# A hybrid retention and attention block on one core: made products dealt over heads and pairs, output weights loaded ahead

## The chip, the core and the metric

One core of a Trainium2 chip runs the whole kernel. The metric is the device time of one execution in microseconds (us), the median over runs.

## What is computed

One layer of an encoder block on 1024 positions and 16 meta tokens put before them (T = 1040), width 1024, all in float32. Cut to what matters:

```python
u = rms_norm(h, pre_w)
rq, rk, rv, rg, aq, ak, av, ag, gr, ga = split(u @ w_in)         # 1024 -> 7680
# branch A: retention, 4 heads, key size 128, value size 256, chunks of 128
o_r = retention_forward(rq, rk, rv) + retention_backward(rq, rk, rv)   # two scans over chunks
y_r = (group_norm(o_r) * ret_nw * silu(rg)) @ w_rb
# branch B: attention in a window of +-128, 8 heads in 2 groups, meta keys always seen, a sink logit
y_a = (softmax_attention(rotary(aq), rotary(ak), av, sink) * silu(ag)) @ w_ab
out = (sigmoid(gr) * y_r + sigmoid(ga) * y_a) @ w_o
return h + rms_norm(out, post_w)                                  # meta tokens dropped
```

## The kernel before

Every float32 product is three TensorE matmuls (`mm3`, lines 69 to 73): each operand is split into a high part (a rounded copy, by ACT or POOL) and a low part (the rest, by VectorE, `dve_lo`), and high x high, low x high and high x low add up in one PSUM bank. So each new operand costs a copy and a VectorE subtraction before TensorE can use it.

The program runs through these stages:

1. The keys and queries of head 0 (`qk0_mm`), while the input loads.
2. Retention, heads 0 to 3 (`retention`). For each chunk `stage1` projects the values (`pv`), transposes keys (`tr`), and `stage2` makes the inner product (`pa`), the chunk's state (`pkv`) and the forward scan (`Sf`). Then a loop runs back over the chunks: the backward state `Sb` is split by POOL and VectorE, one product `pb` uses it, VectorE adds it to the output and takes the statistics of the group norm, and `finish` turns the normed chunk (`to`). While this runs, `fill` gives out pieces of other work, one call of 8 pieces in each backward chunk. A piece is one step of a projection's sum, mostly three matmuls. For heads 0 to 2 these are the next head's key and query projections (`gen_qk`, 48 pieces); for head 3 the first attention keys, products, and attention queries.
3. Attention in four pairs of heads (`attention(hp, fill)`, `hp` 0 to 3), eight blocks of 128 queries each. For a block, `stage1` makes two scores (`ps`; the last matmul of each goes into the list `scored`), softmax runs over VectorE, ACT and POOL, `stage2` turns the probabilities (`pt`), `stage3` multiplies by the values (`po`). After `stage2(n)`, `fill(FILL[hp][n])` gives out pieces: query projections of this pair and the next (`gen_aq`), keys of the second group (`gen_ak`), and products.
4. Four large products by a scheme with 7 instead of 8 half-size products per pair of output blocks: z (gates, 16 units `u`), r and a (the two branches), o (output). `run` walks through all their products in one list of jobs; `prepare` splits the operands six jobs (`LEAD`) ahead; `combine` copies or adds results out of their banks (`copy` on ACT, `plus` on VectorE); `hooks` are functions called after a certain job: `refill` loads and splits the right-hand operand of the next phase, and `pre_split(k)` forms four differences of blocks of the output weights, splits them and stores them for phase o.

**Made products.** `PRE` says which products of the z phase are made early, as filling: product 2, and for some units 3. `gen_pre(u)` loads the weights into `wr` tiles, forms the difference for product 3 with three VectorE operations (`we`, lines 709 to 711), splits (`weh`, `wel`), and then gives 4 pieces of three 128x512 matmuls for each product (`pe`), copies it out and stores it in `e_d`. The z phase loads it back and adds it, and skips the job. Before, there are 22 such products. `all_pre` is one generator, `pre`, for all; `pieces(pre, n)` gives out the next n pieces. In the kernel before, heads 1 to 3 take them by `between`, called in `stage2` behind the forward product of chunks 0 to 3; head 3 takes 16 more by `fill`; pair 3 takes the rest.

**What sets the order.** Instructions are put in order for each engine by a scheduler that works on the traced program with its own estimate of times; each engine then runs its list in that order. `tc.issue_after(ins)` puts the instructions of its block that run on `ins`'s engine behind `ins`. Tiles are rings: a tag with `bufs=n` has n buffers, and a new tile waits until the readers of the one n before it are done. PSUM has 8 banks: 3 for projections and products (`pj`), 2 `p1` (transposes), 2 `p2` (scores, `pkv`), 1 `p3` (`pa`, `pb`, `po`). SP issues nearly all DMAs, in order.

Of the kernel before, what the change touches and what calls it, by code (L numbers as in the profile page):

```python
# [8 lines left out]
R = mybir.dt.float32r  # L9
AF = mybir.ActivationFunctionType  # L10
ALU = mybir.AluOpType
# [11 lines left out]
PIECES = [(0, 272), (272, 528), (528, 784), (784, 1040)]  # L23
HALVES = [(16, 528), (528, 1040)]
MW = 416
FILL = {**{h: (8, 8, 0, 8, 8, 8, 8, 0) for h in range(3)}, 3: (16, 16, 0, 14, 10, 8, 8, 0)}
PRE = {u: (2, 3) if u > 7 else (2,) for u in range(2, 16)}

U_QK, U_V, U_G = 0, 4, 8
U_AK, U_AV, U_AQ, U_AG = 12, 13, 14, 18  # L30
# [8 lines left out]
def block_kernel(ctx: ExitStack, tc: tile.TileContext, xT, x, w_in, w_rb, w_ab, w_out, vecs, dec, sink,  # L39
                 post_w, rope, tab, out):  # L40
    nc = tc.nc
# [198 lines left out]
    with tc.tile_pool(name="setup", bufs=1, reuse_waits="tile") as st:  # L240
# [61 lines left out]
        for k in range(KT):  # L302
            t = xr[k]
# [127 lines left out]

    pend = []

    def retention(h, fill, between):
        q, kt = qk[h]
        qh, ql = [], []
        for i in range(2):
# [62 lines left out]
        def stage2(c):  # L500
            n, vh, vl, kd, s = st1.pop(c)
            if c > 0:
                fh, fl = state["fs"]
                pa = p3(f"pa{h}_{c}")
                mm3(pa[:, 0:256], s[0], s[1], vh, vl, True, True)
                mm3(pa[:, 256:512], qs(qh, c), qs(ql, c), fh, fl, True, True)
                o = op[c - 1]
                nc.scalar.activation(o, pa[:, 0:256], AF.Copy, scale=rcol[:, c:c + 1])
                nc.vector.scalar_tensor_tensor(o, pa[:, 256:512], qdf(h, c), o, op0=ALU.mult, op1=ALU.add)
            if kd:  # L510
                pk = p2(f"pkv{h}_{c}")
            if "f" in kd:
                a, b = kd["f"]
                forward = mm3(pk[:, 0:256], a[0:n], b[0:n], vh[0:n], vl[0:n], True, True)
                if h and c < 4:

                    with tc.issue_after(forward):
                        between(h // 3 + 1)
                new = rp.tile([P, 256], F32, tag="S", bufs=2, name=f"Sf{h}_{c}")
                if c == 0:  # L520
                    nc.vector.tensor_copy(new, pk[:, 0:256])
                else:
                    nc.vector.scalar_tensor_tensor(new, state["f"], cdf(h), pk[:, 0:256], op0=ALU.mult, op1=ALU.add)
                state["f"] = new
                state["fs"] = split_state(new, f"f{h}_{c}")
            if "b" in kd:
                a, b = kd["b"]
                mm3(pk[:, 256:512], a, b, vh, vl, True, True)
                nc.scalar.copy(kvb[c - 1], pk[:, 256:512])
# [150 lines left out]
            nc.vector.tensor_tensor(x[o], x[a], x[b], ALU.subtract)  # L680
            nc.sync.dma_start(xs_d[n][k], x[o])

    def pre_split(k, tile_, src):

        x = {}
        for i, j in ((0, 0), (0, 1), (1, 1), (1, 0)):
            x[i, j] = t = gtile(f"w{i}{j}{k}")
            src(t, 4 * i + k, j)
        for n, o, a, b in SUMS:
            nc.vector.tensor_tensor(x[o], x[a], x[b], ALU.subtract)  # L690
            h, l = (tile_(f"w{n}{k}{e_}", s, R) for s, e_ in enumerate("hl"))
            nc.scalar.copy(h, x[o])
            nc.sync.dma_start(pre_d[n][0][:, k], h.bitcast(F32))
            dve_lo(l, x[o], h)
            nc.sync.dma_start(pre_d[n][1][:, k], l.bitcast(F32))

    gates = [U_G + u for u in range(4)] + [U_AG + u for u in range(4)] + [U_GR + u for u in range(8)]

    def gen_pre(u):
# [29 lines left out]
    def pieces(gen, n):  # L729

        for _ in range(n):
            yield next(gen)
# [9 lines left out]
        decay_table((0,))  # L742
        evac_qk0(3, 5)
    for h in range(NH):
        fill, drain = filler([*([gen_qk(h + 1)] if h < 3 else [gen_ak(0), pieces(pre, 16), gen_aq(0, 0)])])
        if h == 0:
            with tc.issue_after(normed):
                nc.vector.tensor_tensor(qd, rcol[:, 1:9].unsqueeze(1).to_broadcast([P, 2 * NH, NB]),
                                        dtab[:, 8:16].unsqueeze(2).to_broadcast([P, 2 * NH, NB]), ALU.mult)
        with tc.issue_after(rotated):  # L750
            retention(h, fill, filler([pieces(pre, (0, 4, 4, 8)[h])])[0])
            drain()
    while pend:
        pend.pop(0)()
# [19 lines left out]
    def gtile(name):  # L774
        return gp.tile([P, 512], F32, tag="g", bufs=6, name=name)
# [6 lines left out]
    class Phase:  # L782
# [96 lines left out]
        def combine(self, u, p, st):  # L879
            def new(tag):  # L880
                return (lp if tag == "c1" else yp).tile([P, 512], F32, tag=tag, bufs=2, name=f"{tag}{self.nm}{u}")

            def copy(tag):
                st[tag] = new(tag)
                nc.scalar.copy(st[tag], st["X"][0])  # L885

            def plus(o, i, at):
                nc.vector.tensor_tensor(o, i, st[at][0], add)
                return o

            def done(at):
                free.append(st[at][1])

            apart, early = u in self.apart, u in self.early
            if p == 1:
                copy("c1")
                e = self.e.pop((u, 2), None)
                if e is not None:
                    nc.vector.tensor_tensor(st["c1"], st["c1"], e, add)
                    self.post(u, 0, 0, st["c1"])  # L900
            elif p == 6 and (u, 3) in self.e:
                st["u2"] = new("u2")
                plus(st["u2"], self.e.pop((u, 3)), "X")
                self.post(u, 0, 1, plus(st["u2"], st["u2"], "Y"))
            elif p == 2:
                self.post(u, 0, 0, plus(st["c1"], st["c1"], "Z"))
                done("Z")
            elif p == 6:
                copy("u2")
                if (self.nm, u) == last[:2]:  # L910
                    plus(st["u2"], st["u2"], "Y")
                if apart:
                    done("X")
                    st["u3"] = plus(new("u3"), st["u2"], "W")
                if early:
                    plus(st["u2"], st["u2"], "V")
                    done("V")
                    self.post(u, 0, 1, plus(st["u2"], st["u2"], "Y"))
            elif p == 7 and not apart:
                copy("u3")  # L920
                if (self.nm, u) == last[:2]:
                    done("X")
            elif p == 3 and (self.nm, u) == last[:2]:
                self.post(u, 0, 1, plus(st["u2"], st["u2"], "V"))
                done("V")
            elif p == 3 and not early:
                self.post(u, 0, 1, plus(new("c5") if apart else st["u2"], st["u2"], "Y"))
                done("Y")
            elif p == 4 and apart:
                self.post(u, 1, 0, plus(st["u2"], st["u2"], "W"))  # L930
                done("W")
            elif p == 4:
                self.post(u, 1, 0, st["X"][0], new("c5"))
                done("X")
            if "u3" in st and "Y" in st and "c22" not in st:
                st["c22"] = plus(new("c5") if (self.nm, u) == last[:2] else st["u3"], st["u3"], "Y")
                self.post(u, 1, 1, st["c22"])
                if early or 3 in self.pre.get(u, ()) or (self.nm, u) == last[:2]:
                    done("Y")
# [20 lines left out]
    def refill(nm, src):  # L960
# [38 lines left out]
        def got(n):  # L999
            return lambda: get_pre(n)  # L1000

        if nm == "z":
            return {-16: [load(0, 0), load(0, 1)], -13: [load(1, 1)], -11: [plain("B22", 1, 1)],
                    -9: [plain("B11", 0, 0)], -7: [t1, load(1, 0)], -5: [t2, t3], -4: [b21], -3: [plain("T3", 0, 1)],
                    -1: [plain("T4", 0, 0)]}
        if nm == "a":
            return {-16: [load(0, 0)], -14: [load(1, 1)], -13: [plain("B11", 0, 0)], -11: [got("T1")],
                    -10: [load(1, 0)], -9: [got("T2")], -7: [plain("B21", 1, 0)], -5: [got("T3")],
# [5 lines left out]
    def run(phases):  # L1014

        jobs = [(ph, u, p) for ph, _ in phases for u, p in ph.seq]
        hooks, i = {}, 0
        for ph, src in phases:
            i += len(ph.seq)
            if src:  # L1020
                hooks.update({i + j: f for j, f in refill(ph.nm, src).items()})
        for k in range(4):
            hooks[10 * k + 30] = [lambda k=k: pre_split(k, stage, act_src(w_out))]
        n = 0
        for i, (ph, u, p) in enumerate(jobs):
            while n < min(i + LEAD, len(jobs)):
                q, u_, p_ = jobs[n]
                q.prepare(u_, p_)
                n += 1
            yield  # L1030
            ph.product(u, p)
            for f in hooks.get(i, ()):
                f()
# [174 lines left out]
    def attention(hp, fill):  # L1208
# [110 lines left out]
        for n in range(NB):  # L1319
# [7 lines left out]
                yield  # L1327
            stage2(n)
            if hp < 3 or n < NB - 2:
                fill(FILL[hp][n])  # L1330
            if hp in (1, 2) and n in (2, 5):
                sum_row(2 * hp - 2 + n // 3)
            if n >= NB - 2:
# [10 lines left out]
                nc.sync.dma_start(out[P * r:P * r + 2 * P], x[P * r:P * r + 2 * P])  # L1344

    def fills(hp):
        l = [gen_aq(hp, 1)]
        if hp == 2:
            l.insert(0, gen_ak(1))
        if hp < 3:  # L1350
            l.append(gen_aq(hp + 1, 0))
        else:
            l.append(pre)
        return l

    del wak[:]
# [112 lines left out]
```

## Time and profile before

| | before |
|---|---|
| median of 3 runs | 1125.66 us (1124.36 to 1126.15) |
| the profiled execution, its own time | 1122.79 us |
| its span, first to last instruction | 1120.5 us |
| mean granted TensorE clock | 0.978 |
| busy: PE / VectorE (DVE) / ACT / POOL | 1077.5 / 887.9 / 510.3 / 217.9 us |

The profile is of one execution. PE is TensorE, PEld its weight loads, DVE VectorE, SPq the queue of SyncE. Matmuls overlap their neighbours, so the sum of their durations is more than the time they take; from start to start is the better measure. The granted clock is the share of TensorE's full clock that the chip let through. Idle time of an engine is listed with what ended it.

### The profile page before, as it was taken

To read this page: it belongs to the slowest core of one execution; us is meant where nothing else is said; L and a number is where in the kernel's file an instruction comes from. 1 tells how busy PE (TensorE), PEld (TensorE's weight loads), DVE (VectorE), ACT (ScalarE), POOL (GpSimd) and SP (SyncE) were. 2 spreads that over 40 slices of the span, in tenths; PEclk is the share of its full clock that TensorE was granted. 3 is DMA by queue.
4 is the path that set the end of the run, shared out by engine and by line. 5 is a ranking of instruction groups with operands and counts; after the bars stand their busy time and mean duration, and the time that the engine had idled before them with its cause. 6 is when DMAs were issued, how large, how long until landed. Compare 5 with 4: busy or idle time off the path is not lost.

```text
span 1120.5 us, 17075 instructions
## 1 busy us (share of the span) xinstructions
PE 1077.5 (96%) x5939; PEld 924.8 (83%) x5939; DVE 887.9 (79%) x1797; ACT 510.3 (46%) x1128; POOL 217.9 (19%) x276
## 2 busy tenths in 40 slices
PE   8998998998999999999998999999999899999997
PEld 7897897997988988987886788878887688787786
DVE  7888579587788498789756798798989989876765
ACT  7141442322432455554567644445555536433442
POOL 3334224133134244432210000000000000010032
PEclk9999799898999999999999999999999999999998
DMA  7111111102124274233524757699995664789463
GB/s 281 38 67 38 39 58 57 48 20 66 49 87 131 66 251 133 73 129 119 191 104 153 242 175 264 183 357 334 327 359 166 249 207 151 234 193 337 147 113 75
DMA packets 84533, 176.73 MB, mean 158 GB/s; under 512 B 8880, under 2 KB 23728, under 8 KB 83632
## 3 DMA queue, kind: packets, MB, share of 16 engines
q1 hardware_dynamic: 80560, 169.09, 44.1%
q0 software_dynamic: 3456, 6.29, 3.7%
q8 instruction: 46, 0.75, 0.3%
q10 hardware_dynamic: 432, 0.28, 0.1%
q14 instruction: 39, 0.32, 0.1%
HBM read 120.57 MB, written 58.20 MB: 160 GB/s over the span
## 4 chain that ended last, share of the span: by engine, by line
PE 50%; DVE 13%; DMA 7%; issue 3%; ACT 3%; SPq 0%; DVEq 0%; POOL 0%; POOLq 0%; ACTq 0%
PE bz L71 4%; PE bz L72 4%; PE bz L73 4%; PE bo L72 2%; PE bo L71 2%; PE bo L73 2%; PE br L72 2%; PE br L73 2%; PE ba L72 2%; PE br L71 2%; PE ba L73 2%; PE ba L71 2%; PE paq L71 2%; PE paq L72 2%; PE paq L73 2%
## 5 line engine op out<-in xcount | busy, mean ns | idle before, releaser
L1106 POOL DMA_DIRECT2D mx_d<-c1a x4 | 3.7, 917 | 405.2 <-DVE c1a L1097 405.2
L71 PE MATMUL bz<-T,lhz 128*128 128x512 f32 x192 | 76.6, 399 | 2.8 <-ACT u3z L885 2.2
L71 PE MATMUL pv<-wh,big 128*128 128x256 f32 x256 | 75.2, 294 | 1.2 <-DVE m_qk L164 1.2
L73 PE MATMUL bz<-T,lhz 128*128 128x512 f32 x192 | 76.3, 398 | 0.0
L72 PE MATMUL bz<-T,llz 128*128 128x512 f32 x192 | 76.2, 397 | 0.0
L73 PE MATMUL pv<-wl,big 128*128 128x256 f32 x256 | 74.9, 293 | 0.0
L72 PE MATMUL pv<-wh,big 128*128 128x256 f32 x256 | 74.7, 292 | 0.0
L72 PE MATMUL bz<-big,llz 128*128 128x512 f32 x168 | 66.7, 397 | 0.0
L71 PE MATMUL bz<-big,lhz 128*128 128x512 f32 x168 | 66.4, 399 | 0.0
L73 PE MATMUL bz<-big,lhz 128*128 128x512 f32 x168 | 66.3, 396 | 0.0
L1255 DVE CUSTOM_DVE_ANT_0 raw<-ps,mask,nsink 128x400 f32<-128x400 f32 (+1 forms) x64 | 37.9, 595 | 25.3 <-ACT p L1258 24.4
L1267 POOL TENSOR_SCALAR p<-p,den 128x400 f32<-128x400 f32 (+1 forms) x60 | 39.6, 674 | 81.4 <-DVE den L1261 66.2
L71 PEld LDWEIGHTS pv<-wh,big 128*128 128x128 f32 x256 | 51.0, 199 | 2.2 <-DVE m_qk L164 1.5
L1258 ACT ACTIVATE p<-raw,nm 128x401 f32<-128x401 f32 (+1 forms) x64 | 38.8, 606 | 28.5 <-PE pt L1284 16.7
L72 PEld LDWEIGHTS pv<-wh,big 128*128 128x128 f32 x256 | 50.8, 198 | 0.8
L72 PE MATMUL paq<-big,wl 128*128 128x512 f32 x128 | 51.0, 398 | 0.0
L71 PE MATMUL paq<-big,wh 128*128 128x512 f32 x128 | 50.8, 397 | 0.0
L73 PE MATMUL paq<-big,wh 128*128 128x512 f32 x128 | 50.7, 396 | 0.0
L73 PEld LDWEIGHTS pv<-wl,big 128*128 128x128 f32 x256 | 50.6, 198 | 0.0
L566 ACT ACTIVATE ost<-to,rnw 128x128 f32<-128x128 f32 x64 | 20.0, 364 | 61.9 <-PE to L561 56.9
L71 PEld LDWEIGHTS bz<-T,lhz 128*128 128x128 f32 x192 | 36.6, 190 | 12.0 <-ACT u3z L885 2.6
L72 PEld LDWEIGHTS bz<-T,llz 128*128 128x128 f32 x192 | 36.6, 191 | 8.5
(631 smaller groups left out, 3691.0 us busy)
## 6 DMA issues: line engine op xcount, KB each, us to landing
wrz<-in_w_in_dram SPq DMA_DIRECT2D x32, 512.0 KB, 5.8
wr<-in_w_in_dram SPq DMA_DIRECT2D x29, 512.0 KB, 3.8
e<-e SPq DMA_DIRECT2D x44, 256.0 KB, 4.2
we<-in_w_in_dram SPq DMA_DIRECT2D x16, 512.0 KB, 3.6
tg<-tg_d SPq DMA_DIRECT2D x32, 256.0 KB, 4.6
T<-preT SPq DMA_DIRECT2D x6, 1024.0 KB, 7.6
oTr_d<-ost SPq DMA_DIRECT2D x16, 256.0 KB, 2.1
xs<-in_xT_dram SPq DMA_DIRECT2D x8, 512.0 KB, 3.5
```

Of the source, the lines that this page charges most:

```text
L71: nc.tensor.matmul(o, ah, bh, start=first, stop=False, **kw)
L72: nc.tensor.matmul(o, al, bh, start=False, stop=False, **kw)
L73: return nc.tensor.matmul(o, ah, bl, start=False, stop=last, **kw).ins
L566: nc.scalar.activation(ost[0][:, e_, w0:w0 + P], to[:, P * e_:P * e_ + P], AF.Copy, scale=rnw[:, 2 * h + e_:2 * h + e_ + 1])
L1106: nc.gpsimd.dma_start(d, to, accum_op=ALU.add)
L1255: nc.vector.tensor_tensor_reduce(raw[e_][:, 1:1 + wid], s[:, 0:wid], mask[:, mo:mo + wid], -SCALE, nsink[:, hd:hd + 1], ALU.add, ALU.min, ...
L1258: nc.scalar.activation(p[:, 0:1 + wid], raw[e_][:, 0:1 + wid], AF.Exp, scale=-1.0, bias=nm_[:, e_:e_ + 1], accum_out=den[:, e_:e_ + 1])
L1267: nc.gpsimd.tensor_scalar(pt[e_][:, 0:wid], pt[e_][:, 0:wid], den[:, e_:e_ + 1], 1.0, op0=ALU.mult, op1=ALU.mult)
```

## The change

- 20 made products instead of 22. `PRE` now holds product 2 of units 2 to 13 and product 3 of units 6 to 13; units 14 and 15 do all 7 products in the z phase.
- In retention `between` is gone. Products follow in the same `fill`: 4, 4 and 8 pieces behind the key and query projections of the next head for heads 0, 1 and 2; 8 for head 3, between keys and queries of attention.
- In attention each pair has its own row in `FILL`, and products in its list: 8, 16, 0 and 32 pieces, for pair 0 and 1 between this pair's queries and the next pair's. Each fill now stands in `tc.issue_after(scored[-5])`, the second score of the block before, once there are five.
- `pre_split` is cut in two. `pre_load(k)` issues the four loads of output weights six jobs before `pre_split(k)`, into the `sg1` ring of 8 buffers (`stage(..., 1)`) instead of the `g` ring of 6. The subtractions stand behind the latest `plus`, which `near` keeps. The hooks come after jobs 16, 28, 40 and 52 (loads) and 22, 34, 46 and 58 instead of 30, 40, 50 and 60.
- `refill` has no branch of its own for z any more; z takes the general one, whose steps lie over the last 16 jobs in another order.

```diff
-FILL = {**{h: (8, 8, 0, 8, 8, 8, 8, 0) for h in range(3)}, 3: (16, 16, 0, 14, 10, 8, 8, 0)}
-PRE = {u: (2, 3) if u > 7 else (2,) for u in range(2, 16)}
+FILL = (6, 5, 5, 5, 5, 5, 5, 4), (6,) * 8, (6, 5, 5, 4, 4, 4, 4, 0), (7, 7, 7, 7, 6, 6, 8)
+PRE = {u: (2, 3) if u > 5 else (2,) for u in range(2, 14)}
...
-                forward = mm3(pk[:, 0:256], a[0:n], b[0:n], vh[0:n], vl[0:n], True, True)
-                if h and c < 4:
-
-                    with tc.issue_after(forward):
-                        between(h // 3 + 1)
+                mm3(pk[:, 0:256], a[0:n], b[0:n], vh[0:n], vl[0:n], True, True)
...
-    def pre_split(k, tile_, src):
-
-        x = {}
+    def pre_load(k, src):
+
+        w[k] = {}
         for i, j in ((0, 0), (0, 1), (1, 1), (1, 0)):
-            x[i, j] = t = gtile(f"w{i}{j}{k}")
+            w[k][i, j] = t = stage(f"w{i}{j}{k}", 1)
             src(t, 4 * i + k, j)
+
+    def pre_split(k, behind):
+
+        x = w.pop(k)
         for n, o, a, b in SUMS:
-            nc.vector.tensor_tensor(x[o], x[a], x[b], ALU.subtract)
-            h, l = (tile_(f"w{n}{k}{e_}", s, R) for s, e_ in enumerate("hl"))
+            with tc.issue_after(behind):
+                nc.vector.tensor_tensor(x[o], x[a], x[b], ALU.subtract)
+            h, l = (stage(f"w{n}{k}{e_}", s, R) for s, e_ in enumerate("hl"))
...
-        fill, drain = filler([*([gen_qk(h + 1)] if h < 3 else [gen_ak(0), pieces(pre, 16), gen_aq(0, 0)])])
+        fill, drain = filler([gen_qk(h + 1), pieces(pre, (4, 4, 8)[h])] if h < 3 else [gen_ak(0), pieces(pre, 8), gen_aq(0, 0)])
...
-            retention(h, fill, filler([pieces(pre, (0, 4, 4, 8)[h])])[0])
+            retention(h, fill)
...
             def plus(o, i, at):
-                nc.vector.tensor_tensor(o, i, st[at][0], add)
+                near[:] = [nc.vector.tensor_tensor(o, i, st[at][0], add).ins]
                 return o
...
-        if nm == "z":
-            return {-16: [load(0, 0), load(0, 1)], -13: [load(1, 1)], -11: [plain("B22", 1, 1)],
-                    -9: [plain("B11", 0, 0)], -7: [t1, load(1, 0)], -5: [t2, t3], -4: [b21], -3: [plain("T3", 0, 1)],
-                    -1: [plain("T4", 0, 0)]}
...
         for k in range(4):
-            hooks[10 * k + 30] = [lambda k=k: pre_split(k, stage, act_src(w_out))]
+            hooks[12 * k + 16] = [lambda k=k: pre_load(k, act_src(w_out))]
+            hooks[12 * k + 22] = [lambda k=k: pre_split(k, near[0])]
...
             if hp < 3 or n < NB - 2:
-                fill(FILL[hp][n])
+                with tc.issue_after(scored[-5]) if len(scored) > 4 else ExitStack():
+                    fill(FILL[hp][n])
...
-        l = [gen_aq(hp, 1)]
+        l = [gen_aq(hp, 1), pieces(pre, (8, 16, 0, 32)[hp])]
         if hp == 2:
             l.insert(0, gen_ak(1))
         if hp < 3:
             l.append(gen_aq(hp + 1, 0))
-        else:
-            l.append(pre)
```

More of the change, by code (lines that the diff above doesn't have):

```diff
@@ L432, in block_kernel, with retention @@
     pend = []
-    def retention(h, fill, between):
+    def retention(h, fill):
         q, kt = qk[h]
@@ L695, in pre_split @@
             nc.sync.dma_start(pre_d[n][1][:, k], l.bitcast(F32))
+    w, near = {}, []
     gates = [U_G + u for u in range(4)] + [U_AG + u for u in range(4)] + [U_GR + u for u in range(8)]
```

## The prediction, made before the changed kernel had run

> **What bounds the kernel now.** I read the page first, for the engine that is never free and for its clock.
>
> ```profile
> span 1120.5 us, 17075 instructions
> PE 1077.5 (96%) x5939; PEld 924.8 (83%) x5939; DVE 887.9 (79%) x1797; ACT 510.3 (46%) x1128; POOL 217.9 (19%) x276
> PE   8998998998999999999998999999999899999997
> PEclk9999799898999999999999999999999999999998
> ```
>
> TensorE is the bound, and both programs hold the same matmuls, so time can only come from two places: microseconds in which PE stands idle, and microseconds in which its clock is granted by half. The PEclk slices show that the second kind sits where the first is. So I cut the span into stretches by the windows view (columns: window and length, then busy us and count of PE, PEld, DVE, ACT, POOL, then the mean granted clock, DMA share, GB/s).
>
> ```profile
> 40.00:98.00 58.00, 58.00 (x442) 55.38 (x442) 47.76 (x118) 16.26 (x48) 22.90 (x28) 1.00 0.10 33
> 98.00:118.00 20.00, 13.52 (x78) 10.42 (x77) 18.80 (x54) 5.12 (x16) 10.92 (x16) 0.74 0.24 79
> 98.00:126.00 28.00, 21.52 (x115) 17.68 (x113) 20.64 (x59) 6.11 (x19) 11.40 (x17) 0.70 0.20 66
> 186.00:206.00 20.00, 16.24 (x91) 14.13 (x90) 12.59 (x35) 5.70 (x18) 4.90 (x8) 0.74 0.15 54
> 264.00:282.00 18.00, 14.55 (x84) 12.59 (x83) 10.68 (x32) 5.13 (x17) 4.25 (x7) 0.81 0.18 58
> 282.00:316.00 34.00, 34.00 (x273) 33.26 (x272) 25.38 (x65) 15.75 (x42) 5.02 (x9) 1.00 0.20 64
> 487.00:556.00 69.00, 67.43 (x366) 56.47 (x365) 58.55 (x114) 34.74 (x90) 19.63 (x21) 1.00 0.43 142
> 582.00:613.00 31.00, 26.23 (x153) 21.85 (x153) 18.55 (x49) 22.80 (x63) 4.71 (x8) 0.94 0.33 113
> 740.00:751.00 11.00, 8.80 (x32) 6.71 (x31) 8.73 (x16) 5.18 (x10) 0.00 (x0) 0.84 1.00 345
> 856.00:890.00 34.00, 29.94 (x120) 23.28 (x119) 32.69 (x55) 19.02 (x34) 0.00 (x0) 0.95 0.68 236
> 890.00:1030.00 140.00, 140.00 (x603) 113.03 (x602) 114.06 (x186) 60.61 (x107) 8.86 (x10) 1.00 0.69 214
> ```
>
> I price a stretch at its idle time plus (1 - clock) times its length, as if PE had work through all of its half-rate time. The tails of heads 0, 1 and 2: 6.5 + 8.4 = 14.9, 3.8 + 5.2 = 9.0, 3.4 + 3.4 = 6.8; 30.7 in all. The last blocks of attention (582 to 613): 4.8 + 1.9 = 6.7. In the z phase (740 to 751): 2.2 + 1.8 = 4.0. From z to r (856 to 890): 4.1 + 1.7 = 5.8. Between these PE is busy throughout at full clock. A 128x512 matmul costs 140 / 603 = 0.232 us; the window 740:751 also gives the smallest dose of half clock, 0.16 x 11 = 1.8 us, drawn by one wait of 2.2.
>
> Now the tail of head 0 in order of time, PE alone (start, duration, instruction; in brackets the idle time before it and what ended it).
>
> ```profile
> 102.91 0.28 PE L71 MATMUL pv<-wh,big 128*128 128x256 f32 x1
> 103.03 0.28 PE L72 MATMUL pv<-wh,big 128*128 128x256 f32 x1
> ...
> 104.99 0.36 PE L71 MATMUL pb<-Shb,qh 128*128 128x256 f32 x1 [1.22 <-DVE rs L591]
> 107.10 0.35 PE L71 MATMUL pb<-Shb,qh 128*128 128x256 f32 x1 [1.29 <-DVE op L585]
> 109.49 0.55 PE L71 MATMUL pb<-Shb,qh 128*128 128x256 f32 x1 [1.80 <-DVE op L585]
> 116.24 0.66 PE L561 MATMUL to<-ident,op 128*128 128x128 f32 x2 [1.30 <-DVE op L593]
> 117.62 0.48 PE L468 MATMUL tr<-ident,kr 128*128 128x128 f32 x1 [0.50 <-ACT ost L566]
> 119.39 0.80 PE L71 MATMUL pe<-big,weh 128*128 128x512 f32 x1
> ```
>
> Value projections (`pv`) run 0.12 us apart, then stop at 103.0; each backward step waits for VectorE; and the made product of that head (`pe`) starts only at 119.39, since `between` put it behind the forward product of head 1. It takes its `pj` bank, one of three, in turn before the third `pv` tile. That is what keeps projections out of the gap.
>
> **The tails.** The change takes `between` away and lets products follow the projections in `fill`. In the order of the new program's matmuls the tail of head 0 holds, from its first `pb` to the first `tr` of head 1, 7 matmuls of a product and 152 of `pv` tiles 0 to 6, where before it held 35 of `pv`: (152 - 35) x 0.12 + 7 x 0.232 = 15.7 us of work pulled forward into a stretch where PE was busy for 13.5 of 20 us and VectorE for 18.8 (98 to 118). PE must then set its pace. For head 1 the work is about the same as before, 19 us, but dealt some 3.3 us to each chunk down to the last; before, the last two chunks had 0.6. For head 2 the order still leaves the last three steps bare. What is left in each I bound by nothing below and by the present loss above. I take idle 1.2, 0.7 and 2.2 and one dose of 1.8 each: 3.0, 2.5, 4.0, together 9.5. Gain 30.7 - 9.5 = 21.2.
>
> What is late next: the forward chunks of the following head find their `pv` done. In the new order four chunks of heads 1, 2, 3 hold 12.5, 9.8 and 8.9 us of PE work. VectorE's share is in the row 282:316, with this group beside it:
>
> ```profile
> L523 DVE SCALAR_TENSOR_TENSOR Sf<-Sf,dtab,pkv 128x256 f32<-128x256 f32 x7 | 3.3, 474 | 0.5 <-PE pkv L73 0.5
> ```
>
> Seven chunks took 25.4 us of VectorE, 3.6 each, of which the factor turns are head 3's alone. So head 3 can wait 4 x 3.6 - 8.9 = 5.5, head 2 some 2.5, head 1 nothing: 0 to 8, I take 4. Retention: -17.2.
>
> **The pairs.** `FILL` deals each pair its share, and `issue_after(scored[-5])` keeps the matmuls of a fill behind the second score of the block before. On PE nothing but the fill stands behind it; no DMA and no VectorE work is held, since the edge binds instructions of that score's engine; the moved pieces hold nothing of POOL's. So preparation of products may run far ahead, and does: in the new VectorE order units 10 to 13 are prepared in the middle of pair two. Its price, from pair two before:
>
> ```profile
> L79 DVE TENSOR_TENSOR wel<-we,weh 128x1024 fp32r<-128x1024 f32 x6 | 7.4, 1235 | 3.9 <-ACT weh L714 3.9
> L710 DVE TENSOR_TENSOR we<-we,we 128x512 f32<-128x512 f32 x6 | 4.6, 774 | 0.1
> L709 DVE TENSOR_TENSOR we<-we,we 128x512 f32<-128x512 f32 x6 | 4.2, 706 | 5.0 <-DMA we<-in_w_in_dram 2.7 <-issue 2.3
> L711 DVE TENSOR_TENSOR we<-we 128x512 f32<-128x512 f32 x6 | 4.1, 685 | 0.1
> L71 PE MATMUL pe<-big,weh 128*128 128x512 f32 x29 | 11.5, 395 | 0.0
> ```
>
> Six units cost VectorE 20.3 us, 3.4 each. Pair two loses its products (about 3 x 29 x 0.232 = 20 us of PE) but keeps four preparations: PE 67.4 - 20 = 47, VectorE 58.6 - 20.3 + 13.6 = 52. VectorE leads by 5, and its in-order waits for `we` (5.0 and 3.9 above) stand in front of PE. I take 4 us of new waits there (0 to 9). At the end, before, four blocks had no fill:
>
> ```profile
> PE ps L71 <- DVE nm L1255: 1.9, 3, 0.8
> PE po L71 <- ACT oa L1313: 1.8, 2, 1.4
> ```
>
> These are PE's waits in 582:613. With 6 pieces in blocks 4 and 5 two bare blocks are left: half of the 1.9, -1. The last 8 pieces and the tail with its 1.4 stay. Pairs: +3 (-6 to +9). Two products (24 x 0.232 = 5.6 us) move from here into the z phase; that is a transfer and no gain, and units 14 and 15 want as many splits there as their preparation took here.
>
> **The output weights.** Before, `pre_split` loads into the six `g` tiles and subtracts at once:
>
> ```profile
> 738.89 0.33 SPq L1072 DMA_DIRECT2D oTa_d<-c1z  x1
> 739.27 0.42 SPq L1042 DMA_DIRECT2D w<-in_w_out_dram  x1
> ...
> 744.35 0.62 ACT L692 CAST wT31h<-w 128x512 fp32r<-128x512 f32 x1 [1.74 <-DVE w L690]
> 744.88 0.58 ACT L885 COPY u3z<-bz 128x512 f32<-128x512 f32 x1
> 745.51 0.50 PE L71 MATMUL bz<-T,lhz 128*128 128x512 f32 x1 [2.20 <-ACT u3z L885]
> ```
>
> The load is issued at 739.27, the subtraction waits for it, the cast on ACT for the subtraction, the evacuation `u3z` queues behind the cast, and PE waits 2.20 for the bank. `pre_load` issues the same four loads six products, 6 x 12 x 0.232 = 16.7 us, earlier, against some 5 us from issue to the cast here. On SP's queue they are passed behind stores of z results, which that lead covers. `issue_after(near[0])` puts the subtractions behind the last `plus`, which is done when its product is. I count the whole 4.0; if the lead fails, 0.
>
> **z to r.** Without its own branch, z takes the general refill, over 14 jobs where the last pair of units had 10. VectorE was 32.7 of 34 us busy there; the same splits now have 4 x 12 x 0.232 = 11 us more, a load of 33 in 45. PE waited for `llr`, a VectorE split:
>
> ```profile
> PE br L72 <- DVE llr L79: 3.6, 2, 2.9
> ```
>
> 5.8 falls to about 1 (0 to 5.8): -4.8.
>
> **The sum.** -17.2 + 3 - 4.0 - 4.8 = -23.0. The profiled execution took 1122.79 (span 1120.5 and 2.3 around it), 2.9 less than the median 1125.66; its own time would be 1099.8, and the median 1102.7.
>
> [...]
>
> **Rivals.** *VectorE holds the tails.* It is busy 18.8 of 20 us in the first tail, and the new order adds splits of `pv` to it. For it: every wait quoted there ends on VectorE or behind it. Against: 40:98 runs PE full with VectorE at 82%. Then half of the 30.7 stays and the forward chunks cost 8: -7.4 + 3 - 8.8 = -13.2, median 1112.5. *The cover is complete:* 3 us stay in the tails, nothing in the chunks, and the pairs give 1: -27.7 - 1 - 8.8 = -37.5, 1088.2.
>
> *Slower: the clock in pairs zero and two.* Fills held behind scores leave PE nothing to run ahead with, and if a block of these pairs leaves PE waiting as 745.51 did, it costs 2.2 + 1.8 = 4.0. Without the pairs' own term the gain is 26.0, so it turns at seven of these 16 blocks; with ten, +14.0, 1139.7. For it: VectorE leads in pair two. Against: the bare blocks before waited 0.8 and 1.4 and the clock in that row fell by 0.06 only.
>
> *No change:* the pairs give back just what the tails win, 1125. That the change does not do what it says I give nothing: the order shows the projections in the tails.
>
> **The numbers.** Forecast 0.60, VectorE holds the tails 0.14, full cover 0.14, slower 0.08, no change 0.04. The runs of this kernel can tell about 0.2% (2.3 us) from nothing. Faster is the first three, 0.88. The range goes from 1090, near full cover, to 1117, past the first rival; above lie 0.12, below some of the full cover.
>
> **What would show it.** Right: in the stretch from the first `pb` of each head to the next head's `tr`, `pv` matmuls between the steps, no wait over 1 us, PEclk near 1.00; no wait for `u3z` over 1 us in z; `llr` gone from PE's waits. Wrong: waits of PE for `op` or `Slb` in the tails of the old size; PE idle for `nm` or `pal` throughout pairs zero and two with PEclk below 0.9; a span that differs in 890:1030's stretch, which nothing here should touch.

## The result, and the profile after

| | before | after |
|---|---|---|
| median | 1125.01 us (1123.32 to 1126.15, 4 runs) | 1106.11 us (1105.92 to 1106.49, 4 runs) |
| profiled execution, its span | 1122.79, 1120.5 us | 1106.49, 1104.7 us |
| mean granted clock | 0.978 | 0.994 |

The ratio is 0.9834, its 95% interval 0.9817 to 0.9851: faster by 1.7%. The forecast was 1102.7 with a range of 1090 to 1117. The profiled execution fell by 16.3 us where the sum said 23.0. The page of the after profile comes first.

```profile
span 1104.7 us, 17067 instructions
PE 1067.4 (97%) x5939; PEld 916.4 (83%) x5939; DVE 875.6 (79%) x1797; ACT 504.1 (46%) x1126; POOL 219.8 (20%) x276
PE   8999999999999989998998999999999999999997
PEclk9999999999999999999999999999999999999999
```

The matmuls are as many as before. The dips of PE in slices 4, 7 and 10, the three tails, are gone, and the clock with them. New dips stand in slices 15 and 19, inside attention, where before all read 9; slice 22 holds attention's last blocks in both. Here is the span cut by windows again: tails of heads 0, 1, 2; pairs zero to three with the last blocks; z; z to r; the untouched stretch. Columns as in the prediction.

```profile
99.00:127.00 28.00, 28.00 (x222) 26.76 (x221) 23.69 (x60) 7.70 (x24) 12.18 (x18) 1.00 0.26 85
171.00:197.00 26.00, 26.00 (x214) 25.20 (x213) 21.89 (x59) 7.31 (x22) 10.86 (x17) 1.00 0.24 81
245.00:271.00 26.00, 23.86 (x193) 22.57 (x192) 20.91 (x61) 6.31 (x20) 10.13 (x16) 1.00 0.33 105
353.00:404.00 51.00, 48.69 (x256) 41.69 (x256) 38.94 (x86) 24.41 (x59) 15.11 (x17) 0.97 0.52 171
404.00:476.00 72.00, 66.92 (x414) 58.88 (x414) 50.42 (x120) 37.49 (x103) 25.69 (x30) 1.00 0.40 128
476.00:533.00 57.00, 52.55 (x293) 44.14 (x291) 44.76 (x99) 28.34 (x75) 19.61 (x21) 1.00 0.36 118
533.00:567.00 34.00, 31.15 (x160) 25.01 (x161) 21.25 (x50) 17.18 (x45) 8.95 (x12) 1.00 0.27 90
567.00:600.00 33.00, 29.60 (x179) 25.24 (x177) 16.51 (x43) 22.27 (x60) 3.52 (x6) 0.95 0.33 114
710.00:727.00 17.00, 17.00 (x75) 13.80 (x74) 16.65 (x29) 9.09 (x16) 0.00 (x0) 1.00 0.92 279
850.00:892.00 42.00, 42.00 (x182) 33.78 (x181) 34.77 (x58) 21.77 (x40) 0.00 (x0) 1.00 0.75 248
874.00:1015.00 141.00, 141.00 (x607) 113.75 (x606) 113.78 (x187) 60.47 (x107) 8.86 (x10) 1.00 0.70 219
```

The first two tails lose nothing now and the third 2.1 us. The z stretch and z to r are full, and the untouched stretch runs as before (141 / 607 = 0.232 us a matmul). But the four pairs now have 2.3, 5.1, 4.5 and 6.3 us of idle PE (pair three is two rows). The kernel before had 1.6 and 4.9 in its last two pairs, and none in its first two:

```profile
336.00:426.00 90.00, 90.00 (x563) 80.84 (x562) 67.34 (x149) 39.48 (x100) 31.85 (x37) 1.00 0.47 154
426.00:487.00 61.00, 61.00 (x391) 55.43 (x390) 49.67 (x112) 33.36 (x90) 26.00 (x28) 1.00 0.30 99
```

In the first tail the cover looks as forecast: projections (`pv`) on both sides of a backward step, 0.12 us from start to start, and no bracket.

```profile
105.92 0.28 PE L73 MATMUL pv<-wl,big 128*128 128x256 f32 x1
106.04 0.28 PE L71 MATMUL pb<-Shb,qh 128*128 128x256 f32 x1
106.16 0.28 PE L72 MATMUL pb<-Shb,ql 128*128 128x256 f32 x1
106.28 0.28 PE L73 MATMUL pb<-Slb,qh 128*128 128x256 f32 x1
106.40 0.28 PE L71 MATMUL pv<-wh,big 128*128 128x256 f32 x1
```

PE's waits over the whole span (total, times, longest) show what took their place:

```profile
PE ps L71 <- DVE nm L1254: 11.6, 16, 2.0
PE po L71 <- ACT oa L1312: 3.5, 5, 1.5
...
PE bz L71 <- ACT u2z L887: 1.1, 2, 0.6
```

`nm` is VectorE's row maximum of a score; when it is done, the bank of that score is free for the next one. Here is the longest of these waits, in order of time on PE:

```profile
411.60 0.28 PE L73 MATMUL po<-pal,vh 128*128 128x256 f32 x1
413.86 0.45 PE L71 MATMUL ps<-kTh,aqh 128*128 128x400 f32 x1 [1.99 <-DVE nm L1254]
...
415.44 0.34 PE L73 MATMUL ps<-kTl,aqh 128*128 128x400 f32 x1
415.62 0.40 PE L71 MATMUL paq<-big,wh 128*128 128x512 f32 x1
```

and VectorE in the same microseconds:

```profile
411.36 0.72 DVE L79 TENSOR_TENSOR aql<-aq,aqh 128x512 fp32r<-128x512 f32 x1 [2.20 <-ACT aqh L625]
412.00 1.21 DVE L79 TENSOR_TENSOR wl<-wr,wh 128x1024 fp32r<-128x1024 f32 x1
...
413.30 0.50 DVE L1254 CUSTOM_DVE_ANT_0 raw<-ps,mask,nsink 128x272 f32<-128x272 f32 x1
```

VectorE first waits 2.20 for a copy of ACT, then splits a query and a weight, and only then takes the maximum. PE stands before the score. Twelve matmuls of a query projection (`paq`), and a product behind them, begin at 415.62, behind both scores.

The five longest of the 16 waits don't all have one cause on VectorE. In three (1.99, 1.61 and 0.90 us) a split stood ahead of the maximum, in one (1.39) a step of the queries' rotary turn, and in one (1.06) VectorE itself waited 1.80 for `p`, the exponentials of ACT. What they share is a PE with nothing else to run.

**Losses by stage.** For a finer account I take the time from one mark to another on PE and subtract the matmuls between them at the pace that each shape has in undisturbed stretches (0.232 us for 128x512, 0.183 for 128x400, 0.118 for 128x256, and so on). Pair one after: 476.3 - 403.8 = 72.5 us hold 65.2 us of matmuls, so 7.3 are lost. What is left counts idle time and half clock alike, and also slow starts in which the profile shows PE busy: of the 31.0 us of the four pairs after, 18.1 are idle time and some 2 half clock.

| lost us | start | retention | pair 0 | pair 1 | pair 2 | pair 3 | z | z to r | rest |
|---|---|---|---|---|---|---|---|---|---|
| before | 12.1 | 36.7 | 0.2 | 0.4 | 3.8 | 8.3 | 7.9 | 6.6 | 3.0 |
| after | 13.9 | 10.8 | 5.1 | 7.3 | 7.7 | 10.9 | 3.9 | 0.4 | 3.7 |

The start ends at the first `pb`, retention at the first score, z at the first matmul of r, z to r two units later; the rest ends with the second unit of o. The differences sum to -15.3, of -15.8 in the span.

### The profile page after: what moved, and what is told of

The parts are those of the page before. It is cut to its first block, busy times and chain, and to the rows that moved or that the text cites. A ratio compares the mean times of both kernels' runs of the same rounds, so it can differ in the third digit from the quotient of the medians.

```text
span 1104.7 us, 17067 instructions
## 1 busy us (share of the span) xinstructions
PE 1067.4 (97%) x5939; PEld 916.4 (83%) x5939; DVE 875.6 (79%) x1797; ACT 504.1 (46%) x1126; POOL 219.8 (20%) x276
## 4 chain that ended last, share of the span: by engine, by line
PE 73%; DVE 10%; DMA 9%; ACT 3%; issue 3%; POOL 1%; SPq 0%; DVEq 0%; POOLq 0%; ACTq 0%
PE bz L71 6%; PE bz L72 6%; PE bz L73 6%; PE pv L71 3%; PE pv L72 2%; PE pv L73 2%; PE br L72 2%; PE br L71 2%; PE br L73 2%; PE bo L72 2%; PE bo L71 2%; PE bo L73 2%; DMA we<-in_w_in_dram 2%; PE ba L72 2%; PE ba L73 2%
## 5 line engine op out<-in xcount | busy, mean ns | idle before, releaser
L71 PE MATMUL pv<-wh,big 128*128 128x256 f32 x256 | 73.9, 289 | 1.2 <-DVE m_qk L164 1.2
L72 PE MATMUL pv<-wh,big 128*128 128x256 f32 x256 | 73.7, 288 | 0.0
L72 PE MATMUL bz<-big,llz 128*128 128x512 f32 x176 | 69.6, 395 | 0.0
L73 PE MATMUL bz<-big,lhz 128*128 128x512 f32 x176 | 69.3, 394 | 0.0
L71 PE MATMUL bz<-big,lhz 128*128 128x512 f32 x176 | 69.3, 398 | 0.0
L71 PEld LDWEIGHTS pv<-wh,big 128*128 128x128 f32 x256 | 49.0, 192 | 1.7 <-DVE m_qk L164 1.5
L72 PEld LDWEIGHTS pv<-wh,big 128*128 128x128 f32 x256 | 49.0, 191 | 0.2
L1257 ACT ACTIVATE p<-raw,nm 128x401 f32<-128x401 f32 (+1 forms) x64 | 38.8, 607 | 16.7 <-PE pt L1283 6.4
L71 PEld LDWEIGHTS bz<-T,lhz 128*128 128x128 f32 x192 | 36.2, 188 | 10.3 <-ACT u2z L887 1.9
L73 PEld LDWEIGHTS bz<-T,lhz 128*128 128x128 f32 x192 | 36.2, 188 | 8.4
```

Source lines behind the costliest of these rows:

```text
L71: nc.tensor.matmul(o, ah, bh, start=first, stop=False, **kw)
L72: nc.tensor.matmul(o, al, bh, start=False, stop=False, **kw)
L73: return nc.tensor.matmul(o, ah, bl, start=False, stop=last, **kw).ins
L1257: nc.scalar.activation(p[:, 0:1 + wid], raw[e_][:, 0:1 + wid], AF.Exp, scale=-1.0, bias=nm_[:, e_:e_ + 1], accum_out=den[:, e_:e_ + 1])
```

## The experiments

The four experiments e1 to e4 stand beside a before of 1125.07 us (1122.37 to 1126.95, 7 runs), e5 to e8 beside 1126.03 (1121.61 to 1127.58, 17 runs), e10 and e11 beside 1124.89 (1120.29 to 1126.26, 7 runs).

| | median us | ratio to before, 95% interval | retention | pair 0 | pair 1 | pair 2 | pair 3 | z | z to r |
|---|---|---|---|---|---|---|---|---|---|
| after | 1106.11 | 0.9834 (0.9817 to 0.9851) | 10.8 | 5.1 | 7.3 | 7.7 | 10.9 | 3.9 | 0.4 |
| e1, no hold | 1090.04 | 0.9692 (0.9673 to 0.9710) | 11.4 | 0.9 | 0.2 | 3.6 | 9.8 | 4.0 | 0.3 |
| e2, old deal, no hold | 1090.88 | 0.9704 (0.9687 to 0.9720) | 9.8 | 0.9 | 1.1 | 6.7 | 8.6 | 5.1 | 0.4 |
| e3, old deal, hold | 1099.39 | 0.9778 (0.9760 to 0.9797) | 9.9 | 6.2 | 8.0 | 12.0 | 2.0 | 2.7 | 0.4 |
| e7, hold in pair 3 | 1100.12 | 0.9779 (0.9759 to 0.9799) | 12.5 | 1.0 | 1.0 | 13.4 | 10.8 | 5.7 | 0.4 |
| e8, looser hold | 1102.46 | 0.9793 (0.9772 to 0.9814) | 11.0 | 1.7 | 7.2 | 6.1 | 11.4 | 5.9 | 0.3 |
| e10, hold in last blocks | 1089.72 | 0.9695 (0.9671 to 0.9719) | 11.2 | 0.7 | 0.8 | 4.1 | 10.1 | 3.6 | 0.3 |
| e4, retention alone | 1095.91 | 0.9748 (0.9726 to 0.9769) | 9.2 | 1.0 | 0.3 | 7.4 | 8.7 | 5.2 | 6.7 |
| e5, weights alone | 1114.31 | 0.9906 (0.9886 to 0.9926) | 35.7 | 0.9 | 0.3 | 4.4 | 8.9 | 2.7 | 3.4 |
| e6, products and refill alone | 1126.73 | 1.0011 (0.9995 to 1.0026) | 35.6 | 0.2 | 0.4 | 5.0 | 9.4 | 15.9 | 2.4 |
| e11, both of these | 1114.11 | 0.9910 (0.9883 to 0.9938) | 35.9 | 0.8 | 0.3 | 5.5 | 9.3 | 2.8 | 0.3 |

The columns on the right are the losses of each one's profiled execution; a stage that the edit doesn't touch differs by up to some 3 us from one execution to another (z reads 2.7 to 5.9 where only attention differs), so differences of that size there are not read. The columns of before are of its execution of 1122.79 us, which is 2.1 to 3.2 below the medians it is compared with here, so gains read from the columns come out smaller than those of the medians.

**The theories.** The pairs lost 18 us more than before. Either the hold, `issue_after(scored[-5])`, costs this by keeping PE's cover behind the scores that wait; or the new deal does, by leaving pairs without products; or the preparation of products that piles up in pair two, as the prediction had it.

**e1: the hold is taken away.** The deal stays.

```diff
-                with tc.issue_after(scored[-5]) if len(scored) > 4 else ExitStack():
-                    fill(FILL[hp][n])
+                fill(FILL[hp][n])
```

> The changed kernel without issue_after(scored[-5]) around the fills of attention; the deal of pieces stays. In the changed kernel the four pairs lose 31 us against the pace of their matmuls, 13 before. Theory 'hold': the edge keeps TensorE from running ahead into the next block's pieces, so each late score is paid; without it 10 to 18 us come back, 1088 to 1096. Theory 'deal': products in pairs 0 and 1 put their preparation (loads, copies, VectorE) in front of the softmax on VectorE's list, whatever TensorE may do; then 1103 to 1108.

1090.04 us: 16.1 below the changed kernel. The pairs by windows (zero, one, two, then pair three's first blocks and last blocks):

```profile
357.00:409.00 52.00, 51.93 (x278) 44.58 (x277) 41.60 (x86) 26.91 (x63) 18.90 (x21) 1.00 0.56 182
409.00:475.00 66.00, 66.00 (x416) 59.60 (x415) 50.73 (x118) 37.54 (x97) 24.83 (x29) 1.00 0.44 144
475.00:538.00 63.00, 61.82 (x340) 52.20 (x339) 52.45 (x109) 34.67 (x88) 20.10 (x23) 1.00 0.39 123
538.00:554.00 16.00, 14.55 (x97) 12.73 (x96) 8.70 (x28) 10.59 (x32) 3.10 (x6) 1.00 0.17 61
554.00:584.00 30.00, 26.19 (x159) 22.19 (x158) 17.51 (x48) 21.87 (x62) 4.70 (x8) 0.94 0.33 112
```

and the wait for `nm` in these stretches, to set beside 11.6:

```profile
PE ps L71 <- DVE nm L1254: 3.6, 7, 0.8
```

Pairs zero and one are full again. VectorE is busier in them than with the hold (50.7 of 66 against 50.4 of 72), and it delays PE no more: while it does other work, PE now has matmuls of the fill to run. In the order of matmuls 14.1 us of products stand in pair two, where the changed kernel has none; they come from pair three's fills, taken early. The hold explains 16.5 of the 18.2 us that the pairs lost.

**e2: the old deal as well, without the hold.**

```diff
-FILL = (6, 5, 5, 5, 5, 5, 5, 4), (6,) * 8, (6, 5, 5, 4, 4, 4, 4, 0), (7, 7, 7, 7, 6, 6, 8)
+FILL = {**{h: (8, 8, 0, 8, 8, 8, 8, 0) for h in range(3)}, 3: (16, 16, 0, 14, 10, 8, 8, 0)}
...
-                with tc.issue_after(scored[-5]) if len(scored) > 4 else ExitStack():
-                    fill(FILL[hp][n])
+                fill(FILL[hp][n])
...
-        l = [gen_aq(hp, 1), pieces(pre, (8, 16, 0, 32)[hp])]
+        l = [gen_aq(hp, 1), pieces(pre, (0, 0, 0, 56)[hp])]
```

> The changed kernel with attention as before: no issue_after in the fills, the old FILL, no products in pairs 0 to 2 and 56 pieces in pair 3. Retention, the weights' loads, the refill and the 20 products stay as changed. Both theories: the pairs' loss falls from 31 to about 13 us: 1106 - 18 = 1088 (1085 to 1094). If it stays above 1100, the loss came to the pairs from outside them (from what retention leaves undone).

1090.88 us; its interval and that of e1 overlap. Without the hold it does not matter for the time in which pair a product stands in the program: the scheduler takes it where there is room.

**e3: the hold with the old deal**: the two lines of e2 in the changed kernel, and the hold kept.

```diff
-FILL = (6, 5, 5, 5, 5, 5, 5, 4), (6,) * 8, (6, 5, 5, 4, 4, 4, 4, 0), (7, 7, 7, 7, 6, 6, 8)
+FILL = {**{h: (8, 8, 0, 8, 8, 8, 8, 0) for h in range(3)}, 3: (16, 16, 0, 14, 10, 8, 8, 0)}
```

> The changed kernel with the old deal (old FILL, products in pair 3 alone) but with the hold, issue_after(scored[-5]). 'Hold': as slow as the changed kernel or slower, 1104 to 1115. 'Deal': as the old pairs, 1088 to 1094.

1099.39 us, between the two ranges that were expected, so neither theory had the size. With the hold pairs zero to two lose 6.2, 8.0 and 12.0, where the same deal without it loses 0.9, 1.1 and 6.7. In pair three the sign turns: 2.0 against 8.6. All products are held back for it: 39.0 us of them stand in pair three, against 14.8 in e2. So with this deal the hold does two things: it starves the pair before, and feeds the last. With the new deal only the first is seen (10.9 in pair three with the hold, 9.8 without).

**e7: the hold in pair three alone.** e3 suggested that this keeps the good half.

```diff
+                with tc.issue_after(scored[-5]) if hp == 3 else ExitStack():
```

> The changed kernel with the hold in pair 3 alone (issue_after(scored[-5]) only where hp is 3). By stages: without any hold pair 3 loses 2.4 + 3.5 us before its tail and 3.8 in it; with the hold and the old deal 0.1 + 0.1 and 1.9. If the hold does good where nothing follows that PE could run ahead into, and harm elsewhere, 1090 - 5 = 1085 (1083 to 1088). If the hold costs in every pair, above 1092.

A miss: 1100.12 us. Pair two loses 13.4, as this window over most of it shows:

```profile
470.00:520.00 50.00, 42.85 (x232) 35.04 (x230) 42.49 (x94) 29.08 (x81) 15.71 (x18) 0.97 0.36 115
```

Pair two has no products of its own in the new deal. Without a hold it takes 14.1 us of pair three's; with pair three held it takes none, and its own matmuls fall to 38.8 us. VectorE is free for 7.5 of the 50 us, so it isn't the bound. The 10 us that this hold costs are lost in the pair ahead of the one that is held.

**e8: a looser hold**, four scores (two blocks) further back.

```diff
+                with tc.issue_after(scored[-9]) if len(scored) > 8 else ExitStack():
```

> The changed kernel with the fills held behind scored[-9] instead of scored[-5], so two blocks further back. 'Room to run ahead': most of the 16 us that the hold costs come back, 1091 to 1099. If any order between fills and scores costs, whatever the distance, 1102 to 1108.

1102.46 us, 3.6 of the 16 back. That is a miss of "room to run ahead" and inside the range of its rival, that any order between fills and scores costs. The wider room helps pair zero (1.7) and pair two a little (6.1), and leaves pairs one and three as they were. In its order pair two holds 3.5 us of products, where e1 has 14.1: without a hold, fills run further ahead than this lets them. The rival fails in its turn in e10, where a hold costs nothing.

**e10: the hold in the last fills alone**, to keep pieces for the bare blocks without taking them from pair two.

```diff
+                with tc.issue_after(scored[-5]) if hp == 3 and n >= 4 else ExitStack():
```

> The changed kernel with the hold left only on the fills of pair three from block four on; all other fills are free. If the hold costs only by keeping later pieces out of earlier blocks, then held late in the last pair it takes little from pair two (which lost 13.4 us when the whole of pair three was held, and 3.6 without any hold) and keeps pieces for the bare blocks at the end, where the version without a hold still loses 3.5 + 3.8 us: about 1087 us, 1086 to 1090. If the free pieces of pair three's first blocks are what pair two needs least and the bare blocks wait for softmax's chain whatever is dealt to them, nothing is gained over the version without a hold: 1090 to 1092. If a hold anywhere starves what lies ahead of it: over 1095 us.

1089.72 us against 1090.04: no difference that the runs can tell. Pair two is no longer starved (4.1), and pair three gains nothing (10.1 against 9.8), though 5.8 us more of products stand in it than in e1 (13.9 against 8.1). PE's waits in the pairs are as short and no fewer:

```profile
PE ps L71 <- DVE nm L1254: 5.0, 10, 0.8
```

So the bare last blocks are not mended by keeping pieces for them in this way; what would is open.

**e4: retention alone.** The kernel before, with `between` removed and its pieces in the projections' `fill`.

```diff
-                if h and c < 4:
-                    with tc.issue_after(forward):
-                        between(h // 3 + 1)
...
+        fill, drain = filler([gen_qk(h + 1), pieces(pre, (4, 4, 8)[h])] if h < 3 else [gen_ak(0), pieces(pre, 16), gen_aq(0, 0)])
```

> The kernel before with one part of the change: between is gone, products follow the projections in fill (4, 4, 8 pieces for heads 0 to 2, 16 for head 3); 22 products, old attention, old weights' loads, old refill. By the two traces retention's loss falls by 26 us; so 1125 - 26 = 1099 (1095 to 1104) if the parts are independent. By the prediction's term alone (-17) 1108. If the tails' gain is partly given back later in pair 3, 1105 to 1112.

1095.91 us, 29.2 below its before. The profiled executions differ by 24.3: retention's column gives 27.5, and some of it is given back elsewhere, most in pair two (3.6). One part of the change does more than the whole.

**e5: the output weights alone**, in the kernel before, with the change's `pre_load` and `pre_split`.

```diff
-            hooks[10 * k + 30] = [lambda k=k: pre_split(k, stage, act_src(w_out))]
+            hooks[12 * k + 16] = [lambda k=k: pre_load(k, act_src(w_out))]
+            hooks[12 * k + 22] = [lambda k=k: pre_split(k, near[0])]
```

> The kernel before with one part of the change: pre_load six jobs ahead into the sg1 ring, pre_split behind the latest plus, hooks at 16/22 + 12 k. Theory 'load on the path': the wait of 2.2 us for u3z and the half clock behind it go, 1125 - 4 = 1121 (1119.5 to 1122.5). Theory 'chance': in the run with retention's part alone the old loads cost the z phase 0.9 us instead of 4.5, so the wait hung on what fell together there; then 1123 to 1126.

1114.31 us, 11.7 below its before and more than expected. The profiled executions differ by 8.8. The z column gives 5.2. Another 3.2 come from z to r, which the prediction gave to the refill alone: PE's wait for `llr` there was 3.6 in all, and is 1.0 with the weights' splits out of the way.

```profile
PE br L72 <- DVE llr L79: 1.0, 1, 1.0
```

**e6: 20 products and the general refill alone.** The weights stay as before.

```diff
-FILL = {**{h: (8, 8, 0, 8, 8, 8, 8, 0) for h in range(3)}, 3: (16, 16, 0, 14, 10, 8, 8, 0)}
-PRE = {u: (2, 3) if u > 7 else (2,) for u in range(2, 16)}
+FILL = {**{h: (8, 8, 0, 8, 8, 8, 8, 0) for h in range(3)}, 3: (16, 16, 0, 10, 6, 8, 8, 0)}
+PRE = {u: (2, 3) if u > 5 else (2,) for u in range(2, 14)}
...
-        if nm == "z":
-            return {-16: [load(0, 0), load(0, 1)], -13: [load(1, 1)], -11: [plain("B22", 1, 1)],
...
```

> The kernel before with 20 made products (units 14 and 15 whole in z, product 3 of units 6 and 7 made) and the general refill for z; pair 3 takes 8 pieces fewer, all else as before. If the refill's crowding of 14 jobs' VectorE work into 10 makes the wait of 2.9 us for llr, the stretch from the last z products to the second pair of r falls from 6.6 to 0.4 us: 1125 - 6 = 1119 (1117 to 1121). If that wait came from the weights' splits or from retention's order, 1123 to 1127.

A miss: 1126.73 us, no change. Z to r fell to 2.4, but z rose from 7.9 to 15.9 (the profiled execution took 4.9 us more than that of before). PE's waits, and below them VectorE's, between 725 and 770 us:

```profile
PE bz L71 <- DVE u2z L888: 3.0, 1, 3.0
PE bz L71 <- ACT lhz L803: 2.8, 2, 2.3
```

```profile
DVE c1z L899 <- DMA e<-e: 2.7, 2, 1.5
DVE u2z L888 <- DMA e<-e: 1.5, 1, 1.5
```

The products made early (`e`) come back late: VectorE waits for `e`, and PE for VectorE's `u2z`. In this stretch the loads of the refill, the weights and `e` run together, and the DMA share of the window is 0.94. But the share isn't what tells e6 from the others. From 730 to 775 us it is 1.00 in the changed kernel and 1.01 in e11 (below), where PE is busy for 45.00 of 45 us, and between 720 and 775 us a load of `e` lands after 5.7 us in the median in all three. What differs is how early the loads are issued: the eight from 725 to 765 us in e6 stand 4.7 to 7.6 us ahead of their use, the same eight in e11 5.4 to 14.9. In e6 the weights' loads take buffers of the `g` ring, from which `e` is allocated too; in e11 they use `sg1`. That this ring holds the loads of `e` back is argued from the code, not tested by itself, and the wait for `lhz` is not explained.

**e11: e5 and e6 together**, the lines of both diffs in the kernel before.

```diff
+PRE = {u: (2, 3) if u > 5 else (2,) for u in range(2, 14)}
...
+            hooks[12 * k + 16] = [lambda k=k: pre_load(k, act_src(w_out))]
+            hooks[12 * k + 22] = [lambda k=k: pre_split(k, near[0])]
```

> The kernel before with the output weights' loads and splits of the change, 20 products instead of 22, and the general refill for z; retention and attention's fills stay as before. The weights alone took 11 us off (1114.3), the 20 products and the refill alone nothing (1126.7), with 10.6 us lost at the end of z where weights' loads and refill met. Theory: the refill needs the weights out of its way; together the stretch from z to r loses some 0.4 to 1 us instead of 3.4 with the weights alone and 6.6 before: 1111 to 1113 us. Rival: the refill's splits, moved into z's last jobs, cost z what they save later whatever the weights do: 1114 to 1118 us.

The time, 1114.11 us, lies outside the expected 1111 to 1113 and is that of e5. The place is as the theory said: z to r loses 0.3 and z 2.8, and neither `llr` nor the waits of e6 are left. The 3.1 us that z to r won over e5 are lost again in small amounts earlier and later (0.7 at the start, 0.2 in retention, 1.4 in the pairs, 0.1 in z, 0.7 in the rest). Whether the two products that attention gave up cost the pairs the 1.4, or single executions just differ by that, these runs don't tell. So the refill does no harm once the weights are out of its way, and what it then is worth in the total stays open between nothing and 3 us.

## Why the prediction was right, and where it wasn't

The direction, the mechanism of the tails and the range held. The sum missed by 7 us, and it did so as two larger errors that partly cancel: the tails gave 7 us more than forecast, and the pairs lost 15 more, outside the bounds of their own term. So that the time fell within the range is in part luck.

| term | predicted us | measured us |
|---|---|---|
| tails of heads 0 to 2 | -21.2 | -28.6 |
| forward chunks | +4 (0 to 8) | +2.7 |
| pairs | +3 (-6 to +9) | +18.2 |
| output weights, z | -4.0 | -4.0 |
| z to r | -4.8 | -6.2 |
| start, rest, end | 0 | +2.1 |

- **The tails**: the mechanism held. The loss left in them was to be 9.5; by the same measure it is 2.1, one stretch of idle time in head 2 with a single wait of 1.3 for `op`, the one wait there above the 1 us that the prediction allowed. No tail drew half clock (1.00 in all three windows), where I had counted three doses, 5.4 us in all. PE stood idle for no more than 1.3 us in any 3.41 us of retention; in the three tails of before it was 1.84 to 2.01 us in the 3.41 us ahead of the clock's fall (last section).
- **Forward chunks**: what retention as a whole gained (25.9) less the tails (28.6) is the measured 2.7; head 3's own steps are in it. In e4 the whole of retention gives 27.5.
- **The pairs are the term that failed.** The sentence was: "On PE nothing but the fill stands behind it; no DMA and no VectorE work is held". That is true and was read the wrong way round: the fill is the cover. I asked what else the hold would delay, not what PE would have left to run while a score waits. I also looked for the price in VectorE's share of pair two (52 against 47), and no window of the pairs shows VectorE as the bound: it is busy 44.8 of 57 there. What counts is the order within a block: a split ahead of a maximum, or a late exponential, delays the score by 1 to 2 us, which only a ready matmul hides. The rival "slower" named this mechanism, "leave PE nothing to run ahead with", at 4.0 us a block and with chance 0.08. The waits came in every pair, but at 0.7 on average (11.6 / 16), and with one half-clock stretch in pair zero (0.97 of 51 us, 1.5 us) instead of one in each block.
- **Output weights**: -4.0 as forecast, and the 2.20 wait for `u3z` is gone. The exact agreement is chance, as z varies by 3 us where nothing in it changed. Nor do the parts add up: in e4 z lost 5.2 instead of 7.9 with the old loads, perhaps because it started at another moment. e4 gives 29.2, e5 11.7, and e2, which has both and the refill, 34.2.
- **Z to r**: the wait for `llr` is gone, and the gain of 6.2 goes 0.4 past the bound of 5.8, which came from a shorter stretch. In e5 about half of it comes with the weights alone.
- **Start**: 1.8 us that no edit explains. The executions of the same first stage come with 11.7 to 12.4 lost (before, e3, e5 to e8, e10, e11) or with 13.5 to 13.9 (after, e1, e2, e4).
- **The rivals**: "VectorE holds the tails" fell: in 99:127 VectorE is busy for 23.69 of 28 us, beside a PE without a gap. "The cover is complete" gave 1088.2 and is close to what e1 measures, 1090.04: with the hold away the tails and the first two pairs do what it said.

## What to carry to other kernels

An edge that keeps filling work behind a point of the main chain holds back the very work that covers that chain's waits: before adding one, ask what the engine would run in the next wait, and look at the stage before the held one too, which can no longer borrow the held pieces. Filling work should be free to be taken early, and dealt by hand only where the scheduler's order is seen to be bad. The worth of an edit's parts need not add up (e4 and e5 against e2), and a part may be worth nothing while another that it depends on is missing (e6), so parts should be measured together and one by one.

## What the runs showed of the hardware

The granted clock fell to half with less idle time of PE ahead (1.56 to 2.89 us) than the 3.41 us or more that it then stayed low, and not at every wait of that size. These are the stretches at half clock in the profiled executions of before and after, from 30 to 1100 us, with PE's idle time in the 3.41 us ahead of each:

| execution | clock 0.50 from, to (us) | length us | PE idle in the 3.41 us ahead, us |
|---|---|---|---|
| before | 107.77, 124.84 | 17.07 | 2.01 |
| before | 193.11, 203.35 | 10.24 | 1.84 |
| before | 271.61, 278.44 | 6.83 | 1.93 |
| before | 609.53, 612.95 | 3.41 | 1.84 |
| before | 746.07, 749.48 | 3.41 | 2.20 |
| before | 886.01, 889.42 | 3.41 | 2.89 |
| after | 36.97, 40.38 | 3.41 | 1.81 |
| after | 395.37, 398.78 | 3.41 | 1.94 |
| after | 596.75, 600.17 | 3.41 | 1.56 |

The length of a wait did not tell by itself where the clock fell. After PE's wait of 1.39 us that ended at 395.23 (after) the clock was 0.50 from 395.37 to 398.78; with the wait of 0.55 that ended at 393.34 the 3.41 us ahead held 1.94 us of idle PE. After the longer wait of 1.99 that ended at 413.86 it was 1.00 until 596.75, though those 1.99 us are more than the idle time ahead of six of the nine falls.

A DMA share near 1 did not by itself hold PE up: with 1.01 over 45 us (e11) PE had no gap, and with 0.94 (e6) it was busy for 39.16 of 45 us, while loads of `e` landed after 5.7 us in the median in both.
